# A hybrid decoder block on one core: weight splits, sums and small steps issued in another order

## The chip, the cores and the metric

The program runs on one core of a Trainium2 chip, which holds eight. A core has an engine for matrix products (TensorE, PE in the profile, with its weight loads as PEld), one for vectors (VectorE, DVE), one for activations (ScalarE, ACT), a general one (GpSimd, POOL), and SyncE (SP), which here only starts transfers. Each runs its own list of instructions in order and waits for the others at semaphores. PSUM, eight banks of 128 x 512 floats, takes the matrix products; everything else lies in SBUF. The metric is the time of one execution in microseconds (us), lower being better.

## The reference

One layer on 1024 tokens of width 1024, all in 32-bit floats:

```python
h = x
h = h + 0.5 * swiglu(rms_norm(h, ffn1_norm), ffn1_w1, ffn1_w3, ffn1_w2)   # 1024 -> 2816 -> 1024
u = rms_norm(h, mix_norm)
proj = u @ w_in                          # q, k, v of 12 heads, pooling input, gates
y_attn = dilated_mixture_attention(q, k, v) @ w_branch_attn
y_pool = multiscale_pool(pz, pool_w, pool_scale) @ w_branch_pool
merged = gates[:, :, 0] * y_attn + gates[:, :, 1] * y_pool
h = h + merged @ w_out
h = h + 0.5 * swiglu(rms_norm(h, ffn2_norm), ffn2_w1, ffn2_w3, ffn2_w2)
return rms_norm(h, final_norm)
```

`swiglu(x, w1, w3, w2)` is `(silu(x @ w1) * (x @ w3)) @ w2`.

## The kernel before

**Numbers in two parts.** Each 32-bit operand is split in a high part, a copy that rounds it (ACT), and a low part, the difference (DVE or POOL). A product is then three matmuls: high by high, high by low, low by high. `Sevens.split` does that for a 128 x 512 piece of weights: the copy is line 303, the difference line 306. In the entries below POOL is asked for the difference; elsewhere every third goes to DVE.

**Seven products.** Every large matrix product is done by blocks of two by two with seven block products in place of eight, so operands are sums and differences of blocks. The sums of the activations are named b11, b21, b22, t1, t2, t3 and t4. `Quad` holds two blocks of weight columns, a part of the product's width; its seven products run in the order 1, 6, 2, 7, 5, 4, 3. Products 1 and 2 need b11 and b21 (the first 512 tokens), 6, 7, 5, 4 and 3 need t2, t3, t1, t4 and b22, which need the second 512 tokens as well. `Quad.operand(m)` issues the sums of weights (m = 6: two on DVE, lines 345 and 347; m = 7: line 351; m = 3: line 356) and the split of operand m; `Quad.run(m)` issues its 12 matmuls (line 314).

**The entries.** There are three: into the first feed-forward part (FFN1), into the mixers' input projection (mix), and into the second (FFN2). While tokens 512 to 1023, four tiles of 128 rows (t = 4 to 7), are normalised, transposed and made into t1 to t4, the PE runs products 1 and 2 of the first pairs, two a tile. `Entry.run` writes this order out by hand. For a tile it issues:

- product i, and the inverse root of the next tile's norm (DVE line 263, POOL line 264);
- the transposes of b22 and b12 and of t3, each to a PSUM bank; their high parts on ACT (382, 398); b11 subtracted on DVE (460); b22's low part (385);
- the split of the operand of product i + 2, the output of product i, and product i + 1 = k;
- the next tile's scaled rows (DVE 267) and their difference for t3 (POOL 430); then t2 and t4 (DVE 441, 445) and the low parts (401 for t1, 385 for t3, 401 for t2, 401 for t4);
- the split of the operand of product k + 2 before t4's low part, the output of product k, and `after`, in which ACT squares the rows of a tile further on (259).

The last tile has another order: it makes t2 first, and it has the sums of operand 7 among its low parts (`more(1)`). `more(0)`, the sums and split of operand 6, is issued at the end of the tile before. PSUM has four banks under the name "acc", which b22, b12, t3 and t2 take in turn, so each transpose of a tile waits until the same bank of the tile before has been read for the last time. The product after the entry, operand 6 with t2, takes the bank of t3.

**Feed-forward.** Two `Quad`s (w1 and w3) make a `Pair`. The pairs with which the entry began (three in FFN1, two in FFN2) are ended in `up`, in an order by hand: for each product the operand two on, the product, the output of the product before, then one step of `parts` of the pair that ended before. `parts` makes the seven sums of the pair's result and sends each to DRAM with a DMA of SP: first the sum on line 582 and four transfers, then, in one step, lines 587, 588 and 592 with three. The pairs between the begun ones and the last are ordered by a planner that has costs for instructions, not by hand. `Down` multiplies by w2, by hand again: for each of its steps `begin` makes the sums of weights (731) and splits both sides (711 on ACT, 715 on DVE or POOL), two steps ahead of the product (753); `add` adds a finished product to h (758).

**The product with w_out** (`step_o`, 14 steps of two blocks, line 1915) has its left sides split by `hi_o` (ACT 1898) and `lo_o` (DVE 1902). Its end overlaps the first transposes of FFN2's entry (`rows_first2`, `lower`, lines 381, 382, 385, 389).

**The end.** The last product of the last `Down` adds to the upper halves of rows 512 to 1023 alone. Their lower halves are ready before it: `low_half(t)` squares them (ACT 2080), adds the norm's epsilon (DVE 2081) and multiplies by the gain (DVE 2082), a tile in each of the first four steps of the last product. After each tile of the last step come the square of the upper half (2087), a sum (DVE 2091), the root (POOL 2092) and the scaling and stores (`send_out`: DVE 2097, ACT 2100).

Of the kernel before, what the change touches and what calls it, by code (L numbers as in the profile page):

```python
# [13 lines left out]
OP = mybir.AluOpType  # L14
# [112 lines left out]
def tile_block(  # L127
# [275 lines left out]
    class Entry:  # L403
# [18 lines left out]
        def run(self, high, after, first=0):  # L422


            X = self.sv.X

            def scaled_rows(t):
                y = high(t, 1)
                t3 = self.sv.half_tile("s", f"t3_{t}")
                gp.tensor_tensor(t3, y[:, HIGHS], y[:, LOWS], op=OP.subtract)  # L430
                return y, t3

            y, t3 = scaled_rows(4)
            for t in range(4, NT):
                i = first + 2 * (t - 4)
                k = i + 1
                last = t == NT - 1
                b11, b21 = (self.low[t - 4][:, c] for c in (LOWS, HIGHS))

                def second():  # L440
                    ve.tensor_tensor(t2, r3.flat, b11, op=OP.add)
                    return Parts(X, "t2", t2, t)

                def fourth():
                    ve.tensor_tensor(t2, t2, b21, op=OP.subtract)
                    return Parts(X, "t4", t2, t)

                self.product(i)
                if not last:
                    high(t + 1, 0)  # L450
                s = Rows(X, "b22", y[:, HIGHS], t)
                p12 = bank("acc", f"x_b12_{t}")
                for j in range(4):
                    c = slice(j * P, (j + 1) * P)
                    pe.transpose(p12[:, c], y[:, c], ident)
                r3 = Rows(X, "t3", t3, t)
                t2 = bank("acc", f"x_t2_{t}")
                if last:
                    r2 = second()
                ve.tensor_tensor(p12, p12, b11, op=OP.subtract)  # L460
                r1 = Parts(X, "t1", p12, t)
                if not last:
                    s.lower()
                self.operand(i + 2)
                self.out(i)
                self.product(k)
                if last:
                    r2.lower()
                    r3.lower()
                    r1.lower()  # L470
                    self.more(1)
                    r4 = fourth()
                    s.lower()
                    r4.lower()
                else:
                    y, t3 = scaled_rows(t + 1)
                    r2 = second()
                    r1.lower()
                    r3.lower()
                    r2.lower()  # L480
                    r4 = fourth()
                    self.operand(k + 2)
                    r4.lower()
                self.out(k)
                after(t)
                if t == NT - 2:
                    self.more(0)


    class Pair:  # L490
# [77 lines left out]
            for _ in self.parts(place):  # L568
                pass

        def parts(self, place=None):

            j, y = self.j, self.y
            lows, highs = slice(0, HALF), slice(HALF, S)
            a11, a21, a12, a22 = (y[0][:, lows], y[0][:, highs], y[1][:, lows], y[1][:, highs])
            def spill(m, src):
                nc.sync.dma_start(self.sums[m][j // 2][:, j % 2, :], src)

            both = (place or row)(f"gb_{self.sv.name}{j}")
            spill(2, a11)  # L580
            spill(3, a22)
            ve.tensor_tensor(both, y[0], y[1], op=OP.add)
            spill(4, both[:, lows])
            spill(1, both[:, highs])
            yield

            ve.tensor_tensor(a21, a21, a11, op=OP.subtract)
            ve.tensor_tensor(a12, a12, a22, op=OP.subtract)
            spill(6, a12)
            spill(5, a21)  # L590
            e = both[:, lows] if place else self.sv.half_tile("u", f"{j}5")
            ve.tensor_tensor(e, a11, a22, op=OP.add)
            spill(0, e)

    def up(sv, sums, between, name, room, begun):

        with tc.manual_schedule():
            last = ORDER[-1]  # L600
            items = [(q, w, m, out) for q in begun for w, out in ((q.A, q.a_out), (q.B, q.b_out))
                     for m in ORDER if m not in (1, 2)]
            then = Pair(sv, len(begun), sums)
            ahead = [(w, m) for _, w, m, _ in items] + [(then.A, m) for m in ORDER[:2]]
            parts, res = [], []
            for k, (q, w, m, out) in enumerate(items):
                ahead[k + 2][0].operand(ahead[k + 2][1])
                res.append(w.run(m))
                if m == last:
                    raws.depth = 6 if q is not begun[-1] else 4  # L610
                if k > 0:
                    p, _, m, out = items[k - 1]
                    out(m, res[k - 1])
                    for g in parts:
                        next(g, None)
                    if p is not q:
                        parts.append(p.parts())
            out = items[-1][3]
            out(last, res[-1])
            for g in parts:  # L620
                for _ in g:
                    pass
            begun[-1].finish()
        for j in range(len(begun), NPAIR - 1):
            q, then = then or Pair(sv, j, sums), None
            for m in ORDER:
                q.a(m)
            if j == NPAIR - 2:
                between()
            for m in ORDER[:-2]:  # L630
                q.b(m)
            if j == NPAIR - 2:
                end = Pair(sv, NPAIR - 1, sums)
                for m in ORDER[:2]:
                    end.A.operand(m)
            for m in ORDER[-2:]:
                q.b(m)
            q.finish()
        d = Down(name, sums, sv.half_tile, end)
        with tc.manual_schedule():  # L640
            items = [(w, m, out) for w, out in ((end.A, end.a_out), (end.B, end.b_out)) for m in ORDER]
            n = len(items)
            res = []
            for k, (w, m, out) in enumerate(items):
                if k + 2 < n:
                    items[k + 2][0].operand(items[k + 2][1])
                if k == 7:
                    d.load(0, tmp)
                    d.load(1, row)
                if k == n - 4:  # L650
                    d.sums_w(0)
                if k == n - 2:
                    raws.back(2)
                    d.sums_w(1)
                res.append(w.run(m, k < n - 1))
                if k == n - 1:
                    d.dp = room()
                    d.load(2)
                    d.begin(0)
                if k > 0:  # L660
                    items[k - 1][2](items[k - 1][1], res[k - 1])
            d.begin(1)
            end.b_out(ORDER[-1], res[-1])
        return d
# [1235 lines left out]
    def lo_o(i):  # L1900
        hi, lo = ops[i]
        ve.tensor_tensor(lo, lefts.pop(i), hi.bitcast(F32), op=OP.subtract)
# [44 lines left out]
    with tc.manual_schedule():  # L1947
# [47 lines left out]
        lo_o(STEPS - 2)  # L1995
        inverse(1)
        scaled2(0)
        hi_o(STEPS - 1)
        inverse(2)
        scaled2(1)  # L2000
        inverse(3)
        scaled2(2)
        scaled2(3)
        lo_o(STEPS - 1)
        step_o(STEPS - 4)
        raws.end = len(raws.pieces)
        raws.depth = 4
# [2 lines left out]
        step_o(STEPS - 3, range(2))  # L2010
        lower(0, r[0])
        lower(1, r[1])
        r.append(rows_first2(2))
        step_o(STEPS - 3, range(2, 4))
        lower(2, r[2])
# [61 lines left out]
    def low_half(t):  # L2077

        y, st = h_tile(f"n4_{t}"), small.tile([P, 4], F32, tag="nlast", name=f"nst_last{t}")
        ac.activation(y[:, LOWS], h[t][:, LOWS], AF.Square, scale=D ** -0.5, accum_out=st[:, 0:1])  # L2080
        ve.tensor_scalar(st[:, 1:2], st[:, 0:1], EPS, None, op0=OP.add)
        ve.tensor_tensor(y[:, LOWS], h[t][:, LOWS], final_gain[:, LOWS], op=OP.mult)
        ends[t] = y, st

    def high_half(t):
        y, st = ends[t]
# [1 line left out]

    def power(t):
        y, st = ends[t]  # L2090
        ve.tensor_tensor(st[:, 2:3], st[:, 2:3], st[:, 1:2], op=OP.add)
        gp.tensor_tensor(st[:, 3:4], st[:, 2:3], mhalf, op=OP.pow)

    def send_out(t):
        y, st = ends.pop(t)
# [7 lines left out]
    def after2(m, t):  # L2103
# [2 lines left out]
            nc.sync.dma_start(out[rows, :], norm_rows(t, final_gain, "n4", own_row))  # L2106
        elif m == len(DOWN) - 2:
            low_half(4 + t)
        elif m == len(DOWN) - 1:
            high_half(4 + t)  # L2110
            if t > 0:
                send_out(3 + t)
            power(4 + t)
            if t == 3:
                send_out(7)
# [97 lines left out]
```

## Time and profile before

| | |
|---|---|
| median of 3 runs | 1952.12 us (1948.19 to 1957.66) |
| profiled execution, its own time | 1955.09 us |
| its span, first to last instruction | 1953.3 us |
| PE busy | 1910.2 us, 98% |
| DVE, ACT, POOL busy | 1337.3, 776.9, 725.2 us |
| mean granted clock of the PE | 0.993 |

Times in the views are microseconds from the start of the span. A row of a timeline gives start, duration, engine, line, operation, output and inputs, count, and, in brackets, how long the engine stood idle before it and what released it. A row of the waits gives who waited for whom, the sum, how often, and the longest. A row of the windows gives the stretch, its length, and the busy time of PE, PEld, DVE, ACT and POOL with counts, the granted clock of the PE (1.00 is full), and the share and rate of the transfers. The entries lie at about 14 to 62 us, 669 to 702 us and 1297 to 1331 us.

### The profile page before, as it was taken

How to read it: one execution, taken by the hardware profiler on the slowest of the kernel's cores; microseconds unless marked ns; L12 is line 12 of the kernel's file. 1: busy time of each engine (PE TensorE's matmuls, PEld its weight loads, DVE VectorE, ACT ScalarE, POOL GpSimd, SP SyncE). 2: the span in 40 equal slices, each digit the busy share in tenths (PEclk: the TensorE clock that was granted, in tenths of full speed). 3: DMA queues.
4: the chain of work that ended last, by engine and by line, in shares of the span. 5: the costliest groups of instructions: out<-in, count | busy, mean ns of one | idle time of the engine just before them, and what ended most of it. 6: DMA issues, size and time to landing. Idle time of an engine off the chain costs nothing. (4 is left out here: it accounts for less than half of the span.)

```text
span 1953.3 us, 24868 instructions
## 1 busy us (share of the span) xinstructions
PE 1910.2 (98%) x8842; PEld 1571.7 (80%) x8842; DVE 1337.3 (68%) x2020; ACT 776.9 (40%) x1395; POOL 725.2 (37%) x555
## 2 busy tenths in 40 slices
PE   8999999999999999999999999999999999999998
PEld 7788888888888877888877878877788888878886
DVE  6777556658676776657775886877666556577777
ACT  6323333333345542334445763263333333333344
POOL 4333333332223344544544365633333333322131
PEclk9999999999999999999999999999999999999999
DMA  4154323336466537664568977642523223454564
GB/s 185 42 195 150 104 87 103 135 114 216 154 231 214 175 92 250 208 231 178 213 244 304 246 240 261 250 167 78 203 97 126 101 86 103 150 193 137 194 210 162
DMA packets 147436, 333.56 MB, mean 171 GB/s; under 512 B 20208, under 2 KB 40944, under 8 KB 145776
## 3 DMA queue, kind: packets, MB, share of 16 engines
q1 hardware_dynamic: 138096, 307.22, 46.5%
q10 hardware_dynamic: 9216, 24.75, 3.5%
q8 instruction: 70, 1.15, 0.2%
q14 instruction: 54, 0.44, 0.1%
HBM read 229.61 MB, written 102.30 MB: 170 GB/s over the span
## 5 line engine op out<-in xcount | busy, mean ns | idle before, releaser
L753 PE MATMUL d_f<-bhi_f,ahi_f 128*128 128x512 f32 x616 | 241.3, 392 | 2.0 <-ACT ahi_f L711 1.6
L753 PE MATMUL d_f<-bhi_f,alo_f 128*128 128x512 f32 x616 | 241.0, 391 | 1.6 <-POOL alo_f L715 1.3
L753 PE MATMUL d_f<-blo_f,ahi_f 128*128 128x512 f32 x616 | 240.4, 390 | 0.0
L715 POOL TENSOR_TENSOR alo_f<-g_f,ahi_f 128x512 fp32r<-128x512 f32 x68 | 96.9, 1441 | 283.9 <-ACT ahi_f L711 283.9
L314 PE MATMUL u_mixm<-xhi_t_mix,wc_mixm 128*128 128x512 f32 x608 | 196.7, 394 | 5.3 <-DVE xlo_t_mix L385 3.2
L314 PE MATMUL u_mixm<-xhi_b_mix,wc_mixm 128*128 128x512 f32 x456 | 149.1, 394 | 3.3 <-DVE y_m L1036 2.0
L314 PEld LDWEIGHTS u_mixm<-xhi_t_mix,wc_mixm 128*128 128x128 f32 x608 | 114.5, 189 | 31.8 <-POOL wc_mixm L306 3.8
L753 PEld LDWEIGHTS d_f<-bhi_f,alo_f 128*128 128x128 f32 x616 | 116.0, 188 | 28.1 <-POOL alo_f L715 2.5
L753 PEld LDWEIGHTS d_f<-bhi_f,ahi_f 128*128 128x128 f32 x616 | 115.9, 188 | 26.5 <-ACT ahi_f L711 2.0
L753 PEld LDWEIGHTS d_f<-blo_f,ahi_f 128*128 128x128 f32 x616 | 116.1, 188 | 24.1
L314 PE MATMUL u_mixm<-xlo_t_mix,wc_mixm 128*128 128x512 f32 x304 | 119.0, 391 | 0.0
L306 POOL TENSOR_TENSOR wc_mixm<-s_mixm,wc_mixm 128x512 fp32r<-128x512 f32 x52 | 74.8, 1439 | 101.6 <-ACT wc_mixm L303 84.3
L314 PEld LDWEIGHTS u_mixm<-xhi_b_mix,wc_mixm 128*128 128x128 f32 x456 | 85.1, 188 | 24.4 <-POOL wc_mixm L306 3.8
L303 ACT ACTIVATE wc_mixm<-s_mixm 128x512 fp32r<-128x512 f32 x76 | 47.7, 629 | 126.3 <-DVE s_mixm L347 44.4
L314 PE MATMUL u_mixm<-xlo_b_mix,wc_mixm 128*128 128x512 f32 x228 | 88.8, 390 | 0.0
L711 ACT ACTIVATE ahi_f<-g_f 128x1024 fp32r<-128x1024 f32 x84 | 81.8, 974 | 2.9 <-DMA g_f<-gs_f 2.9
L306 POOL TENSOR_TENSOR wc_mixm<-raw,wc_mixm 128x512 fp32r<-128x512 f32 x40 | 57.6, 1442 | 66.2 <-ACT wc_mixm L303 62.2
L711 ACT ACTIVATE bhi_f<-s_f2w 128x512 fp32r<-128x512 f32 x55 | 32.7, 627 | 92.2 <-DVE s_f2w L731 84.5
L1915 PE MATMUL wo<-w_o,o_hi 128*128 128x512 f32 x224 | 69.3, 390 | 0.0
L314 PEld LDWEIGHTS u_mixm<-xlo_t_mix,wc_mixm 128*128 128x128 f32 x304 | 57.5, 189 | 11.9
L711 ACT ACTIVATE bhi_f<-s_f1w 128x512 fp32r<-128x512 f32 x55 | 33.0, 630 | 80.4 <-DVE s_f1w L731 75.5
L715 DVE TENSOR_TENSOR alo_f<-g_f,ahi_f 128x1024 fp32r<-128x1024 f32 (+1 forms) x44 | 52.7, 1197 | 7.1 <-ACT ahi_f L711 7.1
(1317 smaller groups left out, 5096.8 us busy)
## 6 DMA issues: line engine op xcount, KB each, us to landing
g_f<-gs_f SPq DMA_DIRECT2D x70, 512.0 KB, 4.6
gs_f<-y_f SPq DMA_DIRECT2D x88, 256.0 KB, 2.1
raw<-in_w2a_dram SPq DMA_DIRECT2D x35, 512.0 KB, 4.0
raw<-in_w2b_dram SPq DMA_DIRECT2D x35, 512.0 KB, 4.2
gs_f<-gb_f SPq DMA_DIRECT2D x46, 256.0 KB, 2.3
raw<-in_w1a_dram SPq DMA_DIRECT2D x22, 512.0 KB, 4.7
raw<-in_w3a_dram SPq DMA_DIRECT2D x22, 512.0 KB, 6.3
raw<-in_w1b_dram SPq DMA_DIRECT2D x22, 512.0 KB, 4.3
```

The costliest lines, as they stand in the source:

```text
L303: ac.activation(w[:, 0], src, AF.Copy)
L306: eng.tensor_tensor(w[:, 1], src, w[:, 0].bitcast(F32), op=OP.subtract)
L314: pe.matmul(p, a, b, start=(start and k == 0 and q == 0), stop=(k == 3 and q == 2), skip_group_check=not start)
L711: ac.activation(hi[:, c], src, AF.Copy)
L715: eng.tensor_tensor(lo[:, d], src[:, o], hi[:, d].bitcast(F32), op=OP.subtract)
L753: pe.matmul(self.banks[m][t], l, r, start=(first and q == 0), stop=(last and q == 2))
L1915: pe.matmul(banks[m][t], l, r, start=(st == 0 and j == 0 and q == 0), stop=(st == 1 and j == 1 and q == 2))
```

## The change

In `Entry.run` the split of the operand of product i + 2 is issued right behind product i, ahead of the tile's transposes, and that of k + 2 right behind product k. `more(0)` is issued in the last tile but one, behind its scaled rows and ahead of t2, in place of behind the tile. In `parts`, for the pairs that the entry began except the last of them, the three later sums come one in each of three products in place of all three in one; their order becomes 588, 587, 592, each followed by its transfer. In the product with w_out the split of the last step's left side is issued behind `lower(1, r[1])`, in place of its high part among the scalings and its low part behind them. At the end, line 2081 goes: the epsilon is added in the sum that replaces line 2091, and the four multiplications of line 2082 (now `low_rows`) are issued together behind the fourth tile's `low_half`.

```diff
@@ Entry.run
                 self.product(i)
                 if not last:
                     high(t + 1, 0)
+                self.operand(i + 2)
                 s = Rows(X, "b22", y[:, HIGHS], t)
...
                 if not last:
                     s.lower()
-                self.operand(i + 2)
                 self.out(i)
                 self.product(k)
+                self.operand(k + 2)
...
                     y, t3 = scaled_rows(t + 1)
+                    if t == NT - 2:
+                        self.more(0)
                     r2 = second()
                     r1.lower()
                     r3.lower()
                     r2.lower()
                     r4 = fourth()
-                    self.operand(k + 2)
                     r4.lower()
                 self.out(k)
                 after(t)
-                if t == NT - 2:
-                    self.more(0)
@@ Pair.parts
-        def parts(self, place=None):
+        def parts(self, place=None, apart=False):
...
-            ve.tensor_tensor(a21, a21, a11, op=OP.subtract)
-            ve.tensor_tensor(a12, a12, a22, op=OP.subtract)
-            spill(6, a12)
-            spill(5, a21)
             e = both[:, lows] if place else self.sv.half_tile("u", f"{j}5")
-            ve.tensor_tensor(e, a11, a22, op=OP.add)
-            spill(0, e)
+            sums = ((6, a12, a12, a22, OP.subtract), (5, a21, a21, a11, OP.subtract), (0, e, a11, a22, OP.add))
+            for m, to, a, b, how in sums:
+                ve.tensor_tensor(to, a, b, op=how)
+                spill(m, to)
+                if apart:
+                    yield
@@ up
-                        parts.append(p.parts())
+                        parts.append(p.parts(apart=True))
@@ product with w_out
         scaled2(0)
-        hi_o(STEPS - 1)
         inverse(2)
...
         scaled2(3)
-        lo_o(STEPS - 1)
         step_o(STEPS - 4)
...
         lower(1, r[1])
+        split_o(STEPS - 1)
         r.append(rows_first2(2))
@@ the end
         ac.activation(y[:, LOWS], h[t][:, LOWS], AF.Square, scale=D ** -0.5, accum_out=st[:, 0:1])
-        ve.tensor_scalar(st[:, 1:2], st[:, 0:1], EPS, None, op0=OP.add)
+        ends[t] = y, st
+
+    def low_rows(t):
+        y, _ = ends[t]
         ve.tensor_tensor(y[:, LOWS], h[t][:, LOWS], final_gain[:, LOWS], op=OP.mult)
-        ends[t] = y, st
...
-        ve.tensor_tensor(st[:, 2:3], st[:, 2:3], st[:, 1:2], op=OP.add)
-        gp.tensor_tensor(st[:, 3:4], st[:, 2:3], mhalf, op=OP.pow)
+        ve.scalar_tensor_tensor(st[:, 1:2], st[:, 2:3], EPS, st[:, 0:1], op0=OP.add, op1=OP.add)
+        gp.tensor_tensor(st[:, 3:4], st[:, 1:2], mhalf, op=OP.pow)
...
             low_half(4 + t)
+            if t == 3:
+                for u in range(4, NT):
+                    low_rows(u)
```

## The prediction

> **What bounds the kernel.** I read the page first, for the shares, then the waits of the PE, longest first.
>
> ```profile
> span 1953.3 us, 24868 instructions
> PE 1910.2 (98%) x8842; PEld 1571.7 (80%) x8842; DVE 1337.3 (68%) x2020; ACT 776.9 (40%) x1395; POOL 725.2 (37%) x555
> ```
>
> The PE is idle for 43 us in all; only that, and a slow PE clock, can be won by moving work. The waits say where:
>
> ```profile
> PE u_f20a L314 <- DVE xlo_t_f L385: 3.2, 1, 3.2
> PE u_f10a L314 <- DVE xlo_t_f L385: 3.2, 1, 3.2
> PE u_mixm L314 <- DVE xlo_t_mix L385: 3.2, 1, 3.2
> ...
> PE u_f21a L314 <- DVE y_f L529: 1.7, 1, 1.7
> PE d_f L753 <- ACT ahi_f L711: 1.6, 1, 1.6
> ...
> PE x_b L381 <- ACT h_again L389: 1.4, 1, 1.4
> ...
> PE u_f11a L314 <- ACT wc_f11b L303: 0.3, 1, 0.3
> PE u_f12a L314 <- ACT wc_f12b L303: 0.3, 1, 0.3
> ```
>
> The first three are one wait, once in each entry: the first product behind it (operand 6, in the bank of t3) stands until t3's low part is made. The others are the begun pairs (0.3, 0.3 and 1.7), the product with w_out (1.4) and the end (1.6). Next the windows, for the clock:
>
> ```profile
> 62.00:65.50 3.50, 3.50 (x9) 2.73 (x10) 3.42 (x5) 2.15 (x4) 1.47 (x2) 0.51 0.00 0
> 1372.30:1376.00 3.70, 3.69 (x16) 3.09 (x17) 1.75 (x3) 2.32 (x4) 2.02 (x2) 1.00 1.05 396
> 1939.30:1943.00 3.70, 3.70 (x11) 2.85 (x11) 2.54 (x7) 1.19 (x5) 0.55 (x1) 0.54 0.00 0
> 1340.00:1936.00 596.00, 593.33 (x2613) 489.73 (x2612) 397.88 (x522) 209.13 (x322) 180.32 (x132) 1.00 0.42 144
> ```
>
> After an entry's stall the granted clock is 0.51 for 3.5 us, a loss of 3.5 x 0.49 = 1.7 us. The 1.6 us at the end cost the same (3.7 x 0.46 = 1.7), the 1.7 us in the begun pairs nothing. In between the PE is busy for 593.33 of 596 us, so what is won before passes on to the end.
>
> **Entries: splits sooner, sums of operand 6 a tile sooner.** The timelines of FFN1's last two tiles, an engine at a time:
>
> ```profile
> 49.24 1.27 DVE L267 SCALAR_TENSOR_TENSOR x<-x,nst,gain_ffn 128x1024 f32<-128x1024 f32 x1
> 50.44 0.69 DVE L441 TENSOR_TENSOR x_t<-x_t,x 128x512 f32<-128x512 f32 x1
> ...
> 54.91 1.78 DVE L345 TENSOR_TENSOR s_f10a<-raw 128x512 f32<-128x512 f32 x1
> ...
> 59.15 0.70 DVE L441 TENSOR_TENSOR x_t<-x_t,x 128x512 f32<-128x512 f32 x1 [1.73 <-ACT xhi_t_f L382]
> ...
> 69.90 0.79 DVE L345 TENSOR_TENSOR s_f10b<-raw 128x512 f32<-128x512 f32 x1
> ```
> ```profile
> 48.24 0.55 POOL L264 TENSOR_TENSOR nst<-nst,mhalf 128x1 f32<-128x1 f32 x1
> 50.01 1.67 POOL L306 TENSOR_TENSOR wc_f12a<-raw,wc_f12a 128x512 fp32r<-128x512 f32 x1 [1.22 <-ACT wc_f12a L303]
> ...
> 54.87 1.28 POOL L306 TENSOR_TENSOR wc_f12b<-raw,wc_f12b 128x512 fp32r<-128x512 f32 x1 [1.95 <-ACT wc_f12b L303]
> ```
> ```profile
> 57.51 0.63 ACT L303 ACTIVATE wc_f10a<-s_f10a 128x512 fp32r<-128x512 f32 x1 [2.23 <-DVE s_f10a L347]
> ```
> ```profile
> 61.95 0.69 PE L314 MATMUL u_f10a<-xhi_t_f,wc_f10a 128*128 128x512 f32 x1 [3.19 <-DVE xlo_t_f L385]
> ```
>
> Now the two sums and their split sit between 54.91, where the tile before has its last low part, and 59.15, where t2 of the last tile begins: ACT stands 2.23 us for line 347 with the high parts behind it, and DVE then 1.73 for those. This 59.15 - 54.91 = 4.24 goes. From 59.15 to the PE's start are 2.80, which stay.
>
> What comes back is the sums in the tile before. DVE's chain of that tile, 267, two sums, 441 and on, now meets POOL's three operations on SBUF: both splits (issued sooner) and t3. The rows say how they meet. Line 345 took 0.79 us alone and 1.78 when POOL's split had begun first; POOL's split took 1.67, not 1.28, when line 267 had. And who waits comes next:
>
> ```profile
> 1915.47 2.38 DVE L731 TENSOR_TENSOR s_f2w<-raw,raw 128x512 f32<-128x512 f32 x2
> ```
> ```profile
> 1915.83 3.18 POOL L715 TENSOR_TENSOR alo_f<-g_f,ahi_f 128x512 fp32r<-128x512 f32 x2 [10.12 <-ACT ahi_f L711]
> ```
>
> Two DVE operations took 2.38 and POOL's two beside them 3.18, not 2 x 1.28: they alternate, while operations with an operand in PSUM (441 at 50.44 beside POOL) keep 0.7. So I take turns, with 1.28 for each of POOL's, 1.20 for line 267 (49.24 to 50.44) and 0.6 for a sum, from 48.79, where POOL has the inverse root: split to 50.07, 267 to 51.27, second split to 52.55, sum to 53.2, t3 to 54.5, sum to 55.1. Line 441 starts at 55.1, 4.66 later than before; 4.24 goes; operand 6 starts 0.4 later. I take the same for mix, whose wait is equal. In FFN2 the low part of operand 6 is DVE's own:
>
> ```profile
> 1326.88 0.69 DVE L306 TENSOR_TENSOR wc_f20a<-s_f20a,wc_f20a 128x512 fp32r<-128x512 f32 x1 [0.76 <-ACT wc_f20a L303]
> ```
>
> There 0.76 + 0.6 more lie in the chain: 1.8 later. The starts make **+2.6**. Bounds: without collisions the sums cost 1.3, and an entry gains 2.9 (7.3 with FFN2's 1.4 taken off); with one more collision in each, of 1.3, it is +6.5. I take the alternation, since both its directions have rows.
>
> The splits sooner give nothing by themselves while DVE sets the end; they let the PE arrive earlier and wait earlier. The transposes of the last tile's b12 must wait for t1's low part of the tile before (401, two 0.6 steps behind 441), now at 56.3:
>
> ```profile
> 54.59 0.60 PE L455 MATMUL x_b<-ident,x 128*128 128x128 f32 x4
> ```
>
> That is 1.7 later than they ran before, and what the splits save the PE is idle time here too. Most of the stall so moves ahead of the entry's last product, and the 3.5 us of half clock run there, under DVE's chain, not in operand 6. Of 3 x 1.7 I take 3 x 1.4 = **-4.2**, since part can reach into operand 6 (bounds -5.1 and, with a second drop, +5.1). Operand 7 is not late: its sum, split and 1.28 on POOL have operand 6's 12 matmuls to hide under. No DMA moves. The splits' buffers (four) hold this product's, the next two and operand 6.
>
> [...]
>
> **Begun pairs' sums spread.** Three runs of parts: two in FFN1, one in FFN2.
>
> ```profile
> 1365.80 1.76 DVE L587 TENSOR_TENSOR y_f<-y_f 128x512 f32<-128x512 f32 x1
> 1367.48 0.68 DVE L588 TENSOR_TENSOR y_f<-y_f 128x512 f32<-128x512 f32 x1
> ...
> 1371.48 0.68 DVE L529 TENSOR_TENSOR y_f<-u_f21a,y_f 128x512 f32<-128x512 f32 x1
> ```
>
> Line 529 empties the bank of product 5, which the PE reuses. Two of three sums now follow it: 2 x 0.6 = 1.2 earlier. The 1.7 becomes 0.5 and FFN1's 0.3s go: **-1.8** (bounds -2.3 and 0). Two transfers on SP come up to 4 us later, ahead of weight loads that DVE reads over 10 us on; I cost them at nothing.
>
> **w_out.** The low part (1902) leaves the front of the four low parts (385):
>
> ```profile
> 1278.76 1.22 DVE L1902 TENSOR_TENSOR o_lo<-o_sum,o_hi 128x1024 fp32r<-128x1024 f32 x1
> 1279.89 2.48 DVE L385 TENSOR_TENSOR xlo_b_f<-x_b,xhi_b_f 128x512 fp32r<-128x512 f32 x4
> ```
> ```profile
> 1281.26 1.26 PE L381 MATMUL x_b<-ident,h_again 128*128 128x128 f32 x8 [1.45 <-ACT h_again L389]
> ```
>
> The transposes that wait 1.45 come 1.1 earlier. The split then stands on ACT and DVE ahead of the next tile's low parts: its own 1.2 on DVE, less the half that DVE gains before it, makes their bank come about 0.7 late (an estimate): **-0.4** (bounds -1.1, +0.7).
>
> **The end.**
>
> ```profile
> 1922.69 0.15 DVE L2081 TENSOR_SCALAR nst_last<-nst_last 128x1 f32<-128x1 f32 x1 [0.20 <-ACT n L2080]
> 1922.77 0.68 DVE L2082 TENSOR_TENSOR n<-h_last,gain_final 128x512 f32<-128x512 f32 x1
> ...
> 1940.32 0.68 DVE L758 SCALAR_TENSOR_TENSOR h_last<-d_f,h_last 128x512 f32<-128x512 f32 x1
> ...
> 1946.62 0.69 DVE L758 SCALAR_TENSOR_TENSOR h_last<-d_f,h_last 128x512 f32<-128x512 f32 x1 [0.40 <-PE d_f L753]
> ...
> 1948.10 0.16 DVE L2091 TENSOR_TENSOR nst_last<-nst_last 128x1 f32<-128x1 f32 x1
> ```
> ```profile
> 1937.51 0.50 PE L753 MATMUL d_f<-bhi_f,ahi_f 128*128 128x512 f32 x1 [1.58 <-ACT ahi_f L711]
> ```
>
> DVE's chain sets the last split. Three times 0.20 + 0.08 + 0.6 = 0.88 leave it; 0.5, an estimate, returns where 731 now meets POOL's low parts in turns as above. The last split is 2.1 earlier, the 1.58 goes with its 1.7 of clock, and the PE ends 3.3 earlier. But the four multiplications, 2.4, now precede the first add of the last step: from 1940.32 it moves by -2.1 - 0.3 + 1.8, to 1939.7. A tile then needs add, square and sum, 1.56 (1946.62 to 1948.10, and 0.08): the fourth add starts at 1944.4, not 1946.62. **-2.1** (bounds -3.3, 0).
>
> **Sum:** 2.6 - 4.2 - 1.8 - 0.4 - 2.1 = -5.9. The execution profiled took 1955.09 around its span of 1953.3, 3.0 above the median of 1952.12; against the median this makes 1946.
>
> **Rivals.** *DVE and POOL hardly collide* (the order falls otherwise by some tenths): one sum late in each entry, 3 x 1.7 - 1.4 gained, 4.2 of clock, the rest as above: -12.2, 1940. For it: in the old order line 267 never waited. Against: the splits now start just ahead of 267. *The stall stays what it was*: starts +2.6, the clock still drops in operand 6, half of the end's gain: -0.7, 1951. For it: 1.6 us of idleness sufficed once. *Slower*: the planner, which orders 15 pairs between the begun and the last ones, puts them otherwise because its times ahead of them moved. A PE gap per pair of 1.1 us decides (5.9 + 9.8, over 15); at 1.5 it is +16.6, 1969. Against: 593.33 of 596 busy, with DVE busy for 397.88.
>
> [...]
>
> **Chances.** Forecast 0.46 (own range 1941 to 1950), few collisions 0.24, stall unchanged 0.20, planner 0.10. Half a per cent, 9.8 us, is about what a measurement tells from no change: faster is below 1942.4. That holds for the second case and 0.12 of the first: 0.36; slower is the last, 0.10; the rest 0.54. The range, 1936 to 1952.5, leaves out the planner and the fringe of the two others.
>
> **What would show it.** Right: lines 345 and 347 ahead of 441 in the last tile but one, one of them near 1.8 us; a new wait of the PE for DVE line 401 at the last tile's transposes; operand 6 at clock 1.00; no 1.6 in front of the last split. Wrong: line 267 at 1.27 and operand 6 two or more us earlier; or gaps between 150 and 440 us.

## The result, and the profile after

| | before | changed |
|---|---|---|
| median of 20 runs each | 1952.99 us (1948.19 to 1957.66) | 1950.68 us (1948.16 to 1954.01) |
| ratio, with its 95% interval | | 0.9987 (0.998 to 0.9994) |
| profiled execution, its own time | 1955.09 us | 1948.48 us |
| its span, mean granted clock | 1953.3 us, 0.993 | 1946.7 us, 0.994 |

The change gains 0.13%, about 2.5 us (1.2 to 3.9, the ratio times 1952), where 5.9 were forecast. The two profiled spans are 6.6 us apart; a good part of that is not the change, as the stages below show. The top of the page after, and then the waits of its PE:

```profile
span 1946.7 us, 24881 instructions
PE 1905.9 (98%) x8842; PEld 1572.2 (81%) x8842; DVE 1347.1 (69%) x2016; ACT 776.4 (40%) x1395; POOL 725.9 (37%) x555
```
```profile
PE x_b L456 <- DVE xlo_t_f L401: 5.9, 2, 3.8
PE u_mixm L314 <- ACT y_m L1025: 2.4, 2, 1.7
...
PE x_b L456 <- DVE xlo_t_mix L401: 2.0, 1, 2.0
PE u_f21b L314 <- ACT u_f L544: 1.7, 1, 1.7
...
PE u_f12b L314 <- ACT u L544: 1.3, 1, 1.3
...
PE u_f21a L314 <- DVE y_f L529: 0.5, 1, 0.5
...
PE x_b L381 <- ACT h_again L389: 0.3, 1, 0.3
```

The three waits of 3.2 us in front of operand 6 are gone. In their place stand two in each entry: the forecast one of the last tile's transposes for line 401 (2.0, 2.0 and 3.8 us), and one that the prediction does not have, of the entry's *last product* for an output on ACT (L544 and L1025: 1.3, 1.7 and 1.7). The small waits went as forecast: 1.7 became 0.5 in FFN2's begun pairs, 1.4 became 0.3 at w_out, and the 1.6 in front of the end's split is not there. Two waits ahead of those are new too (1.2 for an output on ACT, line 520, in FFN1, and 1.3 for POOL's t3 in FFN2); they come with the splits, for the kernel below with the splits alone has them as well, and operand 6 starts earlier there.

The timeline of FFN1's entry, the last tile but one and the last, DVE and POOL of the kernel after:

```profile
48.61 1.27 POOL L306 TENSOR_TENSOR wc_f12a<-raw,wc_f12a 128x512 fp32r<-128x512 f32 x1
...
49.32 1.64 DVE L267 SCALAR_TENSOR_TENSOR x<-x,nst,gain_ffn 128x1024 f32<-128x1024 f32 x1
50.79 1.32 POOL L306 TENSOR_TENSOR wc_f12b<-raw,wc_f12b 128x512 fp32r<-128x512 f32 x1 [0.91 <-POOL wc_f12a L306]
50.89 1.77 DVE L345 TENSOR_TENSOR s_f10a<-raw 128x512 f32<-128x512 f32 x1
52.07 1.72 POOL L430 TENSOR_TENSOR s_f1t<-x 128x512 f32<-128x512 f32 x1
52.69 1.65 DVE L347 TENSOR_TENSOR s_f10a<-s_f10a,raw 128x512 f32<-128x512 f32 x1
54.27 0.68 DVE L441 TENSOR_TENSOR x_t<-x_t,x 128x512 f32<-128x512 f32 x1
...
58.13 0.69 DVE L401 TENSOR_TENSOR xlo_t_f<-x_t,xhi_t_f 128x512 fp32r<-128x512 f32 x1 [0.66 <-ACT xhi_t_f L398]
59.60 0.70 DVE L441 TENSOR_TENSOR x_t<-x_t,x 128x512 f32<-128x512 f32 x1 [0.78 <-ACT xhi_t_f L382]
...
61.57 0.68 DVE L385 TENSOR_TENSOR xlo_t_f<-x_t,xhi_t_f 128x512 fp32r<-128x512 f32 x1
```

POOL's three operations (48.61, 50.79, 52.07) and DVE's three (49.32, 50.89, 52.69) take turns: all of DVE's are long, 1.64, 1.77 and 1.65 us, and line 441 starts at 54.27 in place of 50.44. The same stretch on PE and ACT:

```profile
55.69 0.75 PE L456 MATMUL x_b<-ident,x 128*128 128x128 f32 x4 [2.04 <-DVE xlo_t_f L401]
...
58.64 0.79 PE L314 MATMUL u_f12b<-xhi_b_f,wc_f12b 128*128 128x512 f32 x1 [1.27 <-ACT u L544]
59.23 0.63 PE L314 MATMUL u_f12b<-xlo_b_f,wc_f12b 128*128 128x512 f32 x1
...
63.47 0.40 PE L314 MATMUL u_f10a<-xhi_t_f,wc_f10a 128*128 128x512 f32 x1
```
```profile
57.50 0.60 ACT L398 ACTIVATE xhi_t_f<-x_t 128x512 fp32r<-128x512 f32 x1 [1.92 <-DVE x_t L445]
57.99 0.59 ACT L544 ACTIVATE u<-u_f12b 128x512 f32<-128x512 f32 x1
```
```profile
55.50:59.10 3.60, 2.14 (x9) 1.59 (x10) 2.63 (x5) 1.68 (x5) 0.92 (x1) 0.58 0.00 0
59.10:62.70 3.60, 3.60 (x10) 2.73 (x10) 3.04 (x5) 2.15 (x4) 0.00 (x0) 0.50 0.00 0
62.70:66.00 3.30, 3.30 (x16) 2.70 (x15) 3.21 (x5) 2.16 (x4) 1.52 (x2) 0.97 0.00 0
```

Here is what happened to the gain. Line 544 copies out the bank of product k of the tile before, to which the last product then adds; that product had ended long ago, but on ACT it is queued behind t4's high part, and that waits for DVE (57.50). So the last product starts at 58.64. The granted clock is 0.58 and then 0.50 for two stretches of 3.6 us, not one (FFN2 is alike, mix has one, 0.56 from 698.0 to 701.6), and a matmul takes 0.63 in place of 0.39. The product ends at 63.47. DVE has t3's low part at about 62.2 (61.57 and 0.6), so it is no longer DVE that releases operand 6: it follows the last product without a gap, at full clock (0.40 and 0.39 us a matmul), 1.52 us later than before (61.95). The other entries are alike: DVE has t3's low part at about 701.1 and 1327.5, and operand 6 starts at 702.0 and 1329.3.

The stages of the profiled executions, from the starts of their first matmuls (the first and last start in the views of the tiles u_f10a, u_f13a, u_mixm, wo, u_f20a and u_f22a). "Before again" is a second profile of the kernel before; the other columns are experiments below. From FFN1's first planned pair to mix it is 522.5 to 522.7 in all of them.

| stage, us | before | before again | changed | entries alone | sums alone | splits alone | pool_late |
|---|---|---|---|---|---|---|---|
| start to operand 6, FFN1 | 61.9 | 62.3 | 63.5 | 63.2 | 64.7 | 61.6 | 59.2 |
| to the first planned pair | 84.5 | 84.4 | 81.7 | 82.8 | 82.8 | 83.2 | 82.2 |
| mix's first product to operand 6 | 33.4 | 33.4 | 34.2 | 35.1 | 34.9 | 32.4 | 30.2 |
| to mix's last product | 359.7 | 360.0 | 358.5 | 358.5 | 358.3 | 359.2 | 358.2 |
| attention and pooling (code unchanged) | 138.5 | 137.9 | 135.8 | 135.4 | 135.7 | 136.5 | 138.9 |
| product with w_out | 95.9 | 95.5 | 95.2 | 95.5 | 95.5 | 95.6 | 95.3 |
| its last product to operand 6, FFN2 | 34.3 | 34.2 | 37.8 | 36.7 | 35.9 | 33.7 | 31.4 |
| to the first planned pair | 58.0 | 56.5 | 55.2 | 56.4 | 56.4 | 56.5 | 55.3 |
| to the end | 564.6 | 562.7 | 562.2 | 562.8 | 562.4 | 563.2 | 561.5 |

Attention swings between 135.4 and 138.9 with no edit in it: 2.7 of the 6.6 us between the two profiles are that. And the two profiles of before differ by 1.9 in the last stage and 1.5 in FFN2's begun pairs, for a reason told under the hardware. Verdicts therefore come from the timed ratios, places from the stages. From each entry's start, operand 6 begins 1.5, 0.8 and 3.5 us later in the changed kernel than before, 5.8 together.

### The profile page after: what moved, and what is told of

Its sections match the earlier page's. It is cut to its first block, busy times and chain, and to the rows that moved or that the text cites. A ratio compares the mean times of both kernels' runs of the same rounds, so it can differ in the third digit from the quotient of the medians.

```text
span 1946.7 us, 24881 instructions
## 1 busy us (share of the span) xinstructions
PE 1905.9 (98%) x8842; PEld 1572.2 (81%) x8842; DVE 1347.1 (69%) x2016; ACT 776.4 (40%) x1395; POOL 725.9 (37%) x555
## 3 DMA queue, kind: packets, MB, share of 16 engines
q8 instruction: 70, 1.15, 0.2%
## 5 line engine op out<-in xcount | busy, mean ns | idle before, releaser
L711 ACT ACTIVATE bhi_f<-s_f2w 128x512 fp32r<-128x512 f32 x55 | 32.8, 627 | 89.3 <-DVE s_f2w L731 78.9
L711 ACT ACTIVATE bhi_f<-s_f1w 128x512 fp32r<-128x512 f32 x55 | 32.9, 630 | 80.2 <-DVE s_f1w L731 75.3
```

Source lines behind the costliest of these rows:

```text
L711: ac.activation(hi[:, c], src, AF.Copy)
```

## Experiments

Theory P is the prediction's: DVE's chain releases operand 6 and the half clock runs out beneath it. Theory Q, formed on the profile after: the PE's last product, late behind an output on ACT and slow by the clock, releases it.

**The parts by themselves.** Four kernels, each with some hunks of the diff shown above and the rest as before: Entry.run alone, all but Entry.run, the end alone, and the begun pairs with w_out.

> The kernel before with the edits of Entry.run alone. By the prediction (DVE's chain releases operand 6, the half clock runs out under that chain): operand 6 starts 0.4, 0.4 and 1.8 us later, 4.2 us of clock come back, the time falls by 1.6 us. By the rival formed on the trace after (the PE's own last product, which waits for an output on ACT and then runs at half clock, releases operand 6): operand 6 starts 1.5, 0.8 and 3.5 us later, the 5.1 us of clock are spent in that product, and the time rises by about 1 us (0 to +2).

> The changed kernel with Entry.run as it was: sums of the begun pairs, w_out and the end alone. By the prediction: 1.8 + 0.4 + 2.1 = 4.3 us faster than before. By the rival (the entries cost what the rest gains): 3 to 5 us faster than before, and 1 to 2 us faster than the changed kernel. If it is only 2 us faster than before, the entries are neutral and the rest was oversized.

> The kernel before with the edits of the end alone. By the prediction: 2.1 us faster (bounds 0 and 3.3), no wait of the PE for line 711 in the last steps, first add of the last step after the four multiplications. By the rival (the four multiplications in a row take the place of the stall): less than 1 us.

> The kernel before with the begun pairs' sums spread and the split of the last left side of the product with w_out moved, and nothing else. By the prediction 1.8 + 0.4 = 2.2 us faster: the wait for line 529 in FFN2 falls from 1.7 to 0.5, the 0.3s in FFN1 go, the wait of 1.4 for line 389 falls to 0.3. If the small waits of the begun pairs are made up elsewhere, only the 1.2 of FFN2 and under 1 of w_out are seen in the stages, and the time is within 1 us of before.

| kernel | ratio to before | 95% interval | times 1952, us | forecast |
|---|---|---|---|---|
| entries alone | 1.0008 | 1.0000 to 1.0017 | +1.6 | -1.6 |
| all but the entries | 0.9981 | 0.9972 to 0.9991 | -3.7 | -4.3 |
| end alone | 0.9993 | 0.9984 to 1.0001 | -1.4 | -2.1 |
| begun pairs and w_out | 0.9979 | 0.9968 to 0.9991 | -4.1 | -2.2 |

The entries miss, and with the other sign: they give nothing or cost up to 3.3 us. The rest holds. Operand 6 with the entries alone starts 1.3, 1.7 and 2.4 us later (the stages). Theory Q had 1.5, 0.8 and 3.5, theory P 0.4, 0.4 and 1.8: FFN1 and mix are Q's or beyond it, FFN2 lies between the two, and the time is within Q's 0 to 2. The begun pairs and w_out are the forecast's 2.2 within their interval (1.8 to 6.2), though the middle, 4.1, is nearly twice it; the stages show 1.1 in FFN2's pairs, 0.5 to 0.9 at w_out, and FFN1's pairs at 82.2 where "splits alone", like it without a drop of the clock there, has 83.2.

**The two halves of the entry.** Only the splits sooner (the first diff), and only the sums and split of operand 6 sooner (the second), each against the kernel before:

```diff
                 self.product(i)
...
+                self.operand(i + 2)
...
-                self.operand(i + 2)
                 self.out(i)
                 self.product(k)
+                self.operand(k + 2)
...
-                    self.operand(k + 2)
```
```diff
                     y, t3 = scaled_rows(t + 1)
+                    if t == NT - 2:
+                        self.more(0)
...
-                if t == NT - 2:
-                    self.more(0)
```

> The kernel before with the splits of the operands i + 2 and k + 2 sooner, and nothing else. By the prediction they give nothing by themselves (within 1 us): the PE's waits for POOL's splits in the entries (0.2 to 0.7) go, and the wait in front of operand 6 grows by as much, to about 4. By the rival that they delay ACT's outputs: waits of the PE for ACT in each entry and 1 to 2 us slower.

> The kernel before with the sums and the split of operand 6 in the last tile but one, ahead of t2, and nothing else: the split for the last product then stands behind them and behind t4. By the prediction's sum the sums cost what they save (+0.4, +0.4 and +1.8 us): 2 to 3 us slower, or 2 us faster if the half clock goes. By the rival (the sums put the PE's last product late, and it releases operand 6): slower by 3 to 6 us, the last product starting behind the split of its operand.

Splits alone: 0.9981 (0.9971 to 0.9992), 3.7 us faster. Sums alone: 0.9997 (0.9988 to 1.0005), no difference. Both expectations missed, the second in both of its theories. In sums alone operand 6 does start late, by 2.8, 1.5 and 1.6 us, behind waits of 2.2 for the same output on ACT, as Q has it; but the stages behind it are 1.7, 1.4 and 1.6 shorter, the half clock being spent mostly ahead of operand 6 (no matmul of u_f10a, u_mixm and u_f20a with t1 to t4 takes over 0.52 us there, against 0.63 at half clock). That kernel also differs in one thing that was not meant: the low parts are dealt out by a count of the splits, and with operand 6 split ahead of k + 2 its low part is DVE's in FFN1 and POOL's in FFN2, the reverse of the kernel before. Why the splits are worth something by themselves is in DVE's and POOL's timelines of that kernel:

```profile
51.09 1.34 POOL L306 TENSOR_TENSOR wc_f12b<-raw,wc_f12b 128x512 fp32r<-128x512 f32 x1 [0.90 <-POOL wc_f12a L306]
52.38 1.30 POOL L430 TENSOR_TENSOR s_f1t<-x 128x512 f32<-128x512 f32 x1
...
55.67 0.68 DVE L345 TENSOR_TENSOR s_f10a<-raw 128x512 f32<-128x512 f32 x1
56.38 0.69 DVE L347 TENSOR_TENSOR s_f10a<-s_f10a,raw 128x512 f32<-128x512 f32 x1
```

POOL's split of k + 2, which in the kernel before started at 54.87 just ahead of line 345 (1.78 us), is done at 52.4; line 345 now takes 0.68. Operand 6 starts 0.3, 1.0 and 0.6 earlier. So each half of the change moves its work into the place that the other half uses: splits sooner free the end of the tile, and the sums are then moved out of that free place to where the splits now are. Apart the splits give 3.7 us and the sums nothing clear of noise (between a gain of 2.3 and a loss of 1.0), together they cost 1.6.

**The output on ACT.** The changed kernel with the output of product k ahead of t4, in the last tile but one:

```diff
                     r2.lower()
+                    if t == NT - 2:
+                        self.out(k)
                     r4 = fourth()
                     r4.lower()
-                self.out(k)
+                if t != NT - 2:
+                    self.out(k)
```

> The changed kernel with the output of product k issued ahead of t4 in the last tile but one, so that ACT has it done before it waits for t4. If the last product's wait for that output and its half clock release operand 6: the waits of 1.3, 1.7 and 1.7 us go, operand 6 starts with DVE's low part of t3, 1.2 to 2.2 us earlier in each entry, and the kernel is 3.7 to 5 us faster than the changed one. If DVE's chain alone sets operand 6, as the prediction has it: less than 1 us from the changed kernel, all of it from DVE waiting less for ACT.

0.9972 (0.9961 to 0.9982), 5.5 us faster than before and so about 3.0 faster than the changed kernel. Its waits in FFN1 and FFN2, and its windows, from the last tile's transposes and from operand 6 in FFN1, and from the transposes in FFN2:

```profile
PE x_b L456 <- DVE xlo_t_f L401: 5.9, 2, 3.8
...
PE u_f10a L314 <- DVE xlo_t_f L385: 2.3, 1, 2.3
...
PE u_f20a L314 <- DVE xlo_t_f L385: 0.9, 1, 0.9
```
```profile
56.20:59.80 3.60, 3.54 (x19) 2.99 (x20) 2.61 (x5) 2.02 (x4) 0.79 (x1) 1.00 0.00 0
62.40:66.00 3.60, 3.52 (x15) 2.82 (x16) 3.52 (x5) 2.16 (x4) 1.43 (x2) 1.00 0.00 0
1321.10:1324.60 3.50, 3.50 (x13) 3.17 (x14) 2.52 (x5) 1.95 (x4) 0.00 (x0) 0.54 0.39 129
```

The wait for ACT is gone, the last product starts on time, and DVE releases operand 6 again, 1.0, 1.1 and 2.1 us earlier than in the changed kernel (62.5 against 63.5; 33.1 against 34.2; 35.7 against 37.8). That is theory Q's mechanism, a little under the 3.7 to 5 it expected; P expected less than 1. It does not tell the lateness of the last product from its slow clock: with the wait gone, this profile has no half clock in FFN1 and mix and one stretch of 3.4 us in FFN2 (0.54 from 1321.1).

**The sums on POOL.** The two sums and the low part of operand 6 go to POOL (the low part was POOL's already in FFN1 and mix), the sums behind t3, the split behind the tile (`operand(6)` then splits the sum that is there; mix likewise):

```diff
+        def sums6(self, eng):
+            if len(self.a) < 4:
+                self.get()
+            a11, a12, a21, a22 = self.a
+            self.s1 = self.sv.half_tile("s", f"{self.n}1")
+            eng.tensor_tensor(self.s1, a21, a22, op=OP.add)
+            self.s2 = self.sv.half_tile("s", f"{self.n}2")
+            eng.tensor_tensor(self.s2, self.s1, a11, op=OP.subtract)
...
                     y, t3 = scaled_rows(t + 1)
                     if t == NT - 2:
-                        self.more(0)
+                        self.more(-1)
...
                 self.out(k)
+                if t == NT - 2:
+                    self.more(0)
...
-                     lambda n: first.A.operand((6, 7)[n]))
+                     lambda n: first.A.sums6(gp) if n < 0 else first.A.operand((6, 7)[n], None if n else gp))
```

> The changed kernel with the two sums of operand 6 and its low part on POOL: the sums behind POOL's t3 of the last tile, the split behind the last tile but one. If DVE's chain with its two sums beside POOL's operations makes the new waits of the entries: line 441 of the last tile but one starts some 3.4 us earlier, the PE's waits for line 401 (2.0, 2.0, 3.8) go, operand 6 starts 2 to 4 us earlier in each entry, and the kernel is 8 to 14 us faster than the changed one. If the PE's last product and its clock set it whatever DVE does: under 3 us.

> The kernel of the run above with the output of product k ahead of t4 in the last tile but one as well. If the last product still waits for that output on ACT when DVE's sums are gone, 1 to 3 us faster than the run above; if that wait was only a consequence of the sums, within 1 us of it.

pool_sums: 0.9937 (0.9924 to 0.9950), 12.3 us faster than before and 9.8 faster than the changed kernel, in the range expected of DVE's chain. With the output earlier as well: 0.9951 (0.9938 to 0.9964), 2.7 us less gained, but the intervals overlap, and operand 6 starts at 60.6 against 60.9, 31.6 against 31.6 and 32.9 against 32.8. As these runs go, the wait for ACT was worth removing only as long as the last product set the end. What still held DVE in pool_sums (by the lines of its file: 448 is 441 above, 389 is 382, 392 is 385, 338 the second sum):

```profile
56.43 0.64 ACT L303 ACTIVATE wc_f10a<-s_f10a 128x512 fp32r<-128x512 f32 x1 [0.79 <-POOL s_f10a L338]
56.96 0.58 ACT L389 ACTIVATE xhi_b_f<-x_b 128x512 fp32r<-128x512 f32 x1
57.44 0.59 ACT L389 ACTIVATE xhi_t_f<-x_t 128x512 fp32r<-128x512 f32 x1
...
58.07 0.70 DVE L448 TENSOR_TENSOR x_t<-x_t,x 128x512 f32<-128x512 f32 x1 [2.19 <-ACT xhi_t_f L389]
```

ACT stands for POOL's second sum with the last tile's high parts behind it, and DVE stands 2.19 us for those. So the split was moved behind them, in the last tile:

```diff
                 if last:
+                    self.more(0)
                     r2 = second()
...
-                if t == NT - 2:
-                    self.more(0)
```

> The kernel with the sums of operand 6 on POOL, its split moved once more: behind t3's high part of the last tile, so that ACT does not wait for POOL's sums with the last tile's high parts behind it. In pool_sums DVE stood 2.19 us for those before its last t2. If that is what still holds operand 6: the 2.19 falls to about 0.8, the PE's waits in front of operand 6 (2.1, 2.2, 2.2) to about 0.7, operand 6 starts 1.4 us earlier in each entry, and the kernel is 4 us faster than pool_sums (up to 9 if the clock no longer drops). If the low part of operand 6, now later on POOL, takes the place: within 1.5 us of pool_sums.

0.9915 (0.9901 to 0.9929): 16.6 us faster than before, 4.3 faster than pool_sums, better than both kernels of this document. The timeline and the waits of pool_late:

```profile
56.24 0.65 ACT L303 ACTIVATE wc_f10a<-s_f10a 128x512 fp32r<-128x512 f32 x1
56.41 0.70 DVE L448 TENSOR_TENSOR x_t<-x_t,x 128x512 f32<-128x512 f32 x1 [0.78 <-ACT xhi_t_f L389]
```
```profile
PE u_f20a L314 <- DVE xlo_t_f L392: 0.7, 1, 0.7
...
PE u_f10a L314 <- DVE xlo_t_f L392: 0.7, 1, 0.7
PE u_mixm L314 <- DVE xlo_t_mix L392: 0.7, 1, 0.7
```

Both numbers are the expected ones, 0.8 and 0.7; the 3.2 us that started this case are down to 0.7.

**The clock once more.** Second profiles, without timing, of splits alone and of the kernel before:

> The kernel of splits_alone once more, for its clock: in its first profile the three waits of 3.0 us in front of operand 6 were followed by no half clock at all. If that belongs to the kernel (its order of work), none again; if it is chance of the execution, half clock behind some of the three.

> The kernel before once more, for its clock: in the profile shown, three waits of 3.2 us and one of 1.58 us at the end were each followed by 3.5 us of half clock. If that belongs to the kernel, all four again and operand 6 at 0.5 to 0.7; if it is chance, the 1.58 us at the end may go without, and the length of the half clock differs.

The windows behind the waits, first of the kernel before (operand 6 of FFN1, mix and FFN2, waits of 3.2, 3.1 and 3.2 us, and the end, a wait of 0.9), then of splits alone in this second look (waits of 3.0 each):

```profile
62.20:65.80 3.60, 3.54 (x9) 2.85 (x10) 3.52 (x5) 2.15 (x4) 1.45 (x2) 0.54 0.00 0
702.60:706.20 3.60, 3.57 (x11) 2.88 (x12) 2.97 (x5) 2.42 (x5) 1.49 (x2) 0.67 0.00 0
1330.10:1333.70 3.60, 3.54 (x15) 2.85 (x16) 3.04 (x6) 2.16 (x4) 1.68 (x2) 1.00 0.01 2
1934.80:1938.40 3.60, 3.50 (x14) 2.67 (x15) 3.34 (x7) 0.75 (x3) 0.00 (x0) 1.00 0.00 0
```
```profile
61.50:65.10 3.60, 3.51 (x10) 2.83 (x11) 3.52 (x5) 2.15 (x4) 1.43 (x2) 0.60 0.00 0
700.70:704.30 3.60, 3.56 (x16) 2.86 (x17) 2.98 (x5) 2.42 (x5) 1.48 (x2) 1.00 0.00 0
1325.30:1328.90 3.60, 3.52 (x15) 2.85 (x16) 3.04 (x6) 2.16 (x4) 1.67 (x2) 1.00 0.01 2
```

The same kernel has the drop behind FFN2's wait in one execution and not in the other, and splits alone has one where it had none. So the kernel alone does not decide whether the clock drops; the execution has a part in it.

## Why the prediction was right or wrong

The time, 1950.68, lies in the range, and the class (no difference beyond half a per cent) was the likeliest. That it lies there is owed to the width of the range, which reached up to the rival in which the stall stays; the gain was forecast at 5.9 us and is 2.5, and one term carries that: timed alone the entries miss by 3.2 us, the rest together by 0.6.

**Starts, +2.6: the sum is right, its two terms are not.** From the same landmarks the last tile's line 441 starts later by 0.45 in FFN1 (59.60 against 59.15), 0.15 in mix (698.57 against 699.52, with mix begun 1.1 earlier) and 2.0 in FFN2 (1324.95 against 1327.85, with w_out ended 4.9 earlier): 2.6. In FFN1 the sums cost 3.8 (54.27 against 50.44) in place of 4.66, 0.4 of the difference because line 267 ended at 50.9, not 51.27, and the rest in the turns behind it, each a little shorter than assumed; and the gap that was to go, 4.24, went by 3.4 alone: 0.87 us stay, because ACT makes the high parts of b22 and t3 only behind t4's and behind the output. Two errors of about 0.85 cancel, which is luck. The alternation itself, against which the rival of few collisions stands, is confirmed: both sums waited, 1.77 and 1.65 in place of 0.68.

**The half clock ahead of the last product, -4.2: the step that failed.** It was said to run "under DVE's chain, not in operand 6". Operand 6 did run at full clock (in FFN1 its longest matmul takes 0.40 us), but the clock was lost all the same. The last product stands in the PE's own order ahead of operand 6; begun late by a second wait and run at half clock, it ended after DVE's chain in every entry (63.47 against 62.2 in FFN1). Of the 5.8 us by which operand 6 is later, DVE's starts make 2.6; the other 3.2 are the last product's, and that is the size of the entries' miss. Behind operand 6 the clock came back about as forecast: with the entries alone the stages there are 1.7, 1.2 and 1.6 us shorter. The prediction took operand 6's start from DVE alone and did not follow the PE to the end of its last product. Nor did it follow ACT: the output of product k kept its place, yet what stands in front of it, t4's high part, came 3.8 us later. Out_early shows it: with that wait taken away the end is DVE's again. The bound of "a second drop, +5.1" came near, but had the place wrong, since the half clock stands ahead of operand 6. With both waits it lasted 6.8 us in four of six entries (FFN1 and FFN2 of the changed kernel, mix and FFN2 of entries alone) and 3.4 in two; with the second wait away, in out_early, never more than 3.4. That the second wait prolongs the drop is likely by this, not shown.

**"The splits sooner give nothing by themselves": wrong.** They gave 3.7 us, by the row quoted above (345 at 0.68 in place of 1.78), which shows as 1.9 us of earlier starts. For the rest there may be fewer drops of the clock: one behind the six waits of 3.0 us of its two profiles, 14 behind the 18 of 3.1 to 3.5 us elsewhere; that the shorter wait is the reason is not shown. The 1.78 beside POOL's split stands in the prediction's first timelines.

**Begun pairs, -1.8, and w_out, -0.4: right.** From the last matmul of FFN2's first begun product to the first planned pair it was 43.0 us (1345.7 to 1388.7) and is 41.8 (1342.7 to 1384.5); 1.7 becomes 0.5, 1.4 becomes 0.3 with the new 0.3 behind it.

**The end, -2.1: the mechanism right, the size from one execution's chance.** The stall and its clock went: no half clock from 1329.3 to 1943.6. But the second profile of before has the clock at full (1.00) behind a shorter wait, 0.9, and against it the last stage gains 0.5 (562.7 to 562.2), against the first 2.4. In the profile shown the adds were 6.30 apart (1940.32 and 1946.62), by what the PE gave at half clock; undisturbed the first and the fourth are 4.87 apart in before (1937.65 and 1942.52 in the second profile) and 4.86 after (1934.95 and 1939.81), and then the four multiplications, which do stand ahead of the first add, take most of the gain back:

```profile
1932.55 2.49 DVE L2084 TENSOR_TENSOR n<-h_last,gain_final 128x512 f32<-128x512 f32 x4
1934.95 0.68 DVE L758 SCALAR_TENSOR_TENSOR h_last<-d_f,h_last 128x512 f32<-128x512 f32 x1
```

Timed alone the end gives 1.4 us, with an interval from a gain of 3.1 to a loss of 0.2.

**The rivals.** Few collisions: no, line 267 took 1.64 and operand 6 was later; no run shows its 1.7 us gained in each entry, the runs show a start 1.5, 0.8 and 3.5 us later. The planner: no, 522.5 and 522.6 us from the first planned pair to mix, and no new gaps. The stall stays what it was: nearest, 1951 against 1950.68, but by other means than its own; operand 6 ran at full clock, and at the end the stall and its clock went.

## What to carry to other kernels

The start of a piece of work is the latest of all that it follows, and its own engine's last work is one of them, at the clock that it will have: when a wait is moved ahead of a product, follow that product to its end. Before work is moved into a stretch, write down what the neighbour engine does there on the same memory (two sums beside POOL took 1.77 and 1.65 us here in place of 0.68), and where the change itself moves the neighbour; a move that helps by itself can meet the next one in the same place. Here the chain that was short of DVE's time gained more from handing operations to an idle engine (14.1 us from the changed kernel to pool_late, with two sums, in FFN2 a low part, and the place of one split) than from the change of order.

## What the hardware showed that was not expected

**The drop of the clock behind a wait differs between executions of one kernel.** In eight profiles (both of before, both of splits alone, all but the entries, the end alone, begun pairs and w_out, pool_sums_out) 24 waits of 3.0 to 3.5 us stand in front of operand 6. At 15 of them the granted clock fell to half, each time for 3.4 us, twice for 6.8 (a part of it sometimes inside the wait); at nine it stayed at 1.00. The half clock behind the waits sums to 55 us, so that such a wait costs 55 / 24 / 2 = 1.15 us beside itself, not the 1.7 of one profile. The three waits of 3.8 us were all followed by a drop, the three of 0.7 us in pool_late by none; at the end a wait of 1.58 was, those of 0.9 to 1.4 were not. In between, waits of 2.1 and 2.2 us (pool_sums) were followed by a drop, three times of three, while those of 2.2 and 2.3 us in out_early were not. What decides whether the clock drops behind a wait is not shown.

**DVE's and POOL's operations with all operands in SBUF took longer side by side.** A sum that took DVE 0.68 alone took 1.65 to 1.78 when a POOL operation, of 1.28 to 1.72, had begun before it, and POOL's t3 took 1.72 in place of 1.30 when DVE's sum had (52.07, behind line 345 at 50.89). An estimate from the rows is that the later one stands until the earlier one is done: in the kernel before, POOL's split ends at 54.87 + 1.28 = 56.15, a sum's 0.6 from there leads to 56.75, and line 345 ended at 54.91 + 1.78 = 56.69. Two operations of DVE with an operand in PSUM took no longer beside POOL's (441 at 50.44 and 401 at 52.23 in the kernel before: 0.69 and 0.68, with POOL's from 50.01 and 51.62); the reason is not shown.
